# Splitting the last tile's down stage by tokens, with all weight blocks kept in SBUF

## Chip, cores, metric

The kernel runs on the 8 cores of one Trainium2 chip; each core computes one sequence of the batch. The metric is the device time of the slowest core, in microseconds (us). Executions come in a fast state and in a slow one, in which one die or both show a lower granted TensorE clock.

## The reference

Two layers of a decoder trunk, then one RMSNorm. What matters here is the very end of it:

```python
        y = modulate(rmsnorm(h, norm_g[l, 2]), sh3, sc3)
        h = h + 0.5 * g3[:, None, :] * swiglu(y, ffn2_wg[l], ffn2_wu[l], ffn2_wd[l])
    return rmsnorm(h, final_g)
```

`h` has 4096 positions of 1024 channels. The kernel holds it transposed, as 8 tiles of 512 tokens, each with 8 blocks (KC) of 128 channels. The hidden width 2816 is 22 blocks (FC).

## The kernel before

The program records tasks, a scheduler orders them per engine, and semaphores are emitted from the dependencies. The down stage of a tile is 8 groups of 22 matmuls; each group is followed by a residual add. `norm_out` is the final norm (cut to what matters):

```python
            def downs(self, tiles, dst={}, keep=True, lag=0):
                wd = {}
                for t in dst:
                    load_h(dst[t], t, self.src, self.bsrc, G.M)
                for m in range(KC + lag):
                    if m < KC:
                        wd[m] = load_wd(self.l, self.w, m, G.M)      # ring of 3 slots
                    for n, t in enumerate(tiles):                    # both tiles use the block in turn
                        k = m - lag * n
                        if 0 <= k < KC:
                            self.down(t, k, wd[k][0], wd[k][1], dst.get(t), keep)

        rsR = Ring([NM + 7168], [128, T], F32, "rstd")               # ONE buffer for the reciprocal norm
        # norm_sum: 8 squares (ACT), 7 sums (DVE or POOL), one mean matmul, logarithm, exp -> rs
        def norm_out(ht, t, pos, fine=False):
            rs, brs = norm_sum(ht, pos, 2 if fine else 0)
            for kc in range(KC):
                hk, bh = ht.ap[:, kc, :], ht.b[kc]
                fg = fg_sb[:, kc:kc + 1]
                G.op([dvex(lambda e, hk=hk, fg=fg: e.scalar_tensor_tensor(out=hk, in0=hk, scalar=fg, in1=rs, ...), 680)],
                     reads=[brs, bC["cst"]], writes=[bh], name="fin", pos=pos)
                ...                                                  # output DMA per block (fine) or per two

                # the end of the program
                hts = {6: HT(ACT[0]), 7: HT(ACT[1])}
                fc.downs((6, 7), hts, False, 1)
                norm_out(hts[6], 6, G.M, True)
                norm_out(hts[7], 7, G.M, True)
```

The softmax here doesn't subtract the row's maximum and nothing guards it: scores larger than these inputs give would overflow.

## Time and profile before

| | before |
|---|---|
| three timings | 5432.4, 5211.1, 4849.5 us (the first two slow) |
| profiled run, fast | 4873.3 us |
| from the last gate matmul to the end, die 0 | 169.9 to 170.4 us |
| of it after the last down matmul | 17.5 to 18.1 us |

The third row is read on each core from the end of the last gate matmul to the end of the execution. (A matmul ends its turn where the next one can start, 216 ns after its own start at 512 columns; its record ends some 0.17 us later.) On cores at full clock this stretch agrees to 0.1 us in the change and to 1.1 us in the kernel before, over two profiles of each, whereas the whole time moves by several us with the throttle. The view of spans and granted clocks of the kernel before shows that throttle even in a fast run; die 1, at a clock of 0.990, takes 40 us longer:

```profile
die 0 (median of its cores): 4824.8 us, clock 0.998
die 1 (median of its cores): 4864.5 us, clock 0.990
```

### The profile page before, as it was taken

What the parts mean: (1) busy time and instruction counts of PE and PEld (TensorE: products, weight loads), DVE (VectorE), ACT (ScalarE), POOL (GpSimd) and SP (SyncE); (2) the same over time, 40 slices, a digit from 0 to 9 for tenths busy, and PEclk for the clock granted to TensorE, in tenths of its full rate; (3) what the DMA queues carried; (4) which work ended last, traced back from release to release, by engine and by line L of the source; (5) the groups of instructions that cost most, each with busy time, mean ns of one, the idle gap of its engine ahead of it and who ended that gap; (6) DMA issues with size and microseconds to landing.
All of it is one profiled execution on the core that took longest, in us unless ns stands there. A gap on an engine that the chain in (4) does not pass through costs nothing.

```text
span 4871.8 us, 74168 instructions; the slowest of 8 cores (4820.7 to 4871.8 us)
## 1 busy us (share of the span) xinstructions
PE 4789.6 (98%) x25859; PEld 2257.4 (46%) x25859; DVE 2461.2 (51%) x4088; ACT 2035.0 (42%) x3024; POOL 973.5 (20%) x949
## 2 busy tenths in 40 slices
PE   6999999999999999999999999999999999999998
PEld 2444445444445554444444444444444455544443
DVE  6452566473655473655233326645537544525433
ACT  5112576452755352512211127645537444525311
POOL 0001551212531111300100026312235100122101
PEclk9999999999999999999999999999999999999999
DMA  8888676777575768755721466756665644473314
GB/s 240 169 191 230 166 204 159 191 206 218 172 209 150 200 192 240 218 147 165 249 66 39 120 200 163 208 155 184 149 190 164 185 148 140 123 248 124 136 42 157
DMA packets 370033, 834.80 MB, mean 171 GB/s; under 512 B 148961, under 2 KB 182113, under 8 KB 363234
## 3 DMA queue, kind: packets, MB, share of 16 engines
q1 hardware_dynamic: 352338, 741.56, 49.4%
q0 software_dynamic: 17328, 88.49, 12.1%
q8 instruction: 213, 3.49, 0.3%
q14 instruction: 154, 1.26, 0.1%
HBM read 741.20 MB, written 234.88 MB: 200 GB/s over the span
## 4 chain that ended last, share of the span: by engine, by line
PE 92%; ACT 2%; DMA 2%; DVE 2%; issue 1%; POOL 0%; SPq 0%; DVEq 0%; ACTq 0%; POOLq 0%
PE ps L1002 48%; PE ps L1030 25%; PE ps L1141 9%; PE ps L1467 5%; PE ps L1409 3%; PE ps L1375 2%; DMA arena<-xP 1%; DMA arena<-hS 0%; DVE arena L1206 0%; DVE arena L948 0%; POOL arena L1182 0%; DMA arena<-ada_w 0%; ACT arena L1184 0%; DMA arena<-wdS 0%; PE ps L1234 0%
## 5 line engine op out<-in xcount | busy, mean ns | idle before, releaser
L1002 PE MATMUL ps<-arena 128*128 128x512 bf16 x11264 | 2511.5, 381 | 32.6 <-DMA arena<-wgu 25.0
L1002 PEld LDWEIGHTS ps<-arena 128*128 128x128 bf16 x11264 | 1083.9, 98 | 1312.0 <-issue 86.4
L1030 PE MATMUL ps<-arena 128*128 128x512 bf16 x5632 | 1242.7, 382 | 1.1 <-DMA arena<-wdS 1.1
L1008 ACT ACTIVATE arena<-ps 128x512 f32<-128x512 f32 x704 | 419.7, 597 | 1283.7 <-PE ps L1002 1279.9
L1010 DVE SCALAR_TENSOR_TENSOR arena<-arena,ps 128x512 f32<-128x512 f32 x704 | 481.4, 685 | 771.9 <-ACT arena L1008 770.7
L1030 PEld LDWEIGHTS ps<-arena 128*128 128x128 bf16 x5632 | 550.7, 98 | 665.6 <-issue 47.9
L926 POOL TENSOR_TENSOR arena<-arena 128x512 f32<-128x512 f32 (+2 forms) x351 | 414.2, 1180 | 1218.4 <-ACT arena L919 1116.3
L1034 DVE SCALAR_TENSOR_TENSOR arena<-ps,arena 128x512 f32<-128x512 f32 x256 | 192.1, 751 | 908.3 <-PE ps L1030 899.9
L1015 DVE TENSOR_TENSOR arena<-ps,arena 128x512 bf16<-128x512 f32 x704 | 485.0, 690 | 216.6 <-PE ps L1002 193.3
L1141 PE MATMUL ps<-arena 128*128 128x512 bf16 x2560 | 577.1, 385 | 9.0 <-ACT arena L1225 5.8
L919 ACT ACTIVATE arena<-arena 128x512 bf16<-128x512 f32 x424 | 250.9, 625 | 709.1 <-DVE arena L1034 379.3
L1393 ACT ACTIVATE arena<-ps 128x1024 bf16<-128x1024 f32 (+1 forms) x384 | 344.9, 950 | 308.3 <-PE ps L1375 307.6
L1141 PEld LDWEIGHTS ps<-arena 128*128 128x128 bf16 x2560 | 251.0, 99 | 314.7 <-issue 52.0
L1396 DVE TENSOR_TENSOR arena<-arena 128x1024 bf16<-128x1024 bf16 (+1 forms) x384 | 256.1, 675 | 126.0 <-ACT arena L1393 124.6
L961 ACT ACTIVATE arena<-arena 128x512 bf16<-128x512 f32 x372 | 278.4, 806 | 45.2 <-DVE arena L948 45.1
L1445 POOL TENSOR_TENSOR arena<-arena 64x512 bf16<-64x512 f32 x128 | 163.8, 1280 | 623.1 <-ACT arena L1440 600.0
L948 DVE TENSOR_TENSOR arena<-arena 128x512 f32<-128x512 f32 x384 | 268.3, 747 | 35.0 <-ACT arena L934 32.0
L1467 PE MATMUL ps<-arena 128*128 128x512 bf16 x1024 | 230.1, 386 | 0.0
L1425 DVE TENSOR_TENSOR arena<-ps,arena 128x512 f32<-128x512 f32 x256 | 175.5, 685 | 65.2 <-PE ps L1409 57.5
L1409 PEld LDWEIGHTS ps<-arena 128*128 128x128 bf16 x2736 | 173.6, 98 | 63.4 <-issue 7.1
L1213 POOL TENSOR_TENSOR arena<-arena 128x512 bf16<-128x512 f32 x128 | 167.9, 1320 | 174.8 <-DVE arena L1204 120.2
L1409 PE MATMUL ps<-arena 128*128 128x128 bf16 x2736 | 194.4, 219 | 1.9 <-DVE arena L1010 0.9
(79 smaller groups left out, 2112.7 us busy)
## 6 DMA issues: line engine op xcount, KB each, us to landing
arena<-wguS SPq DMA_DIRECT2D x242, 512.0 KB, 5.7
arena<-hS SPq DMA_DIRECT2D x204, 512.0 KB, 6.8
arena<-wdS SPq DMA_DIRECT2D x128, 704.0 KB, 5.9
arena<-ada_w SPq DMA_DIRECT2D x144, 512.0 KB, 5.9
hS<-arena SPq DMA_DIRECT2D x224, 256.0 KB, 5.8
wguS<-wgu POOLq DMA_DIRECT2D x66, 512.0 KB, 7.8
hS<-arena SPq DMA_DIRECT2D x64, 512.0 KB, 4.3
arena<-xP SPq DMA_DIRECT2D x48, 512.0 KB, 9.0
```

The costliest lines, as they stand in the source:

```text
L926: f = lambda e, a=a, sq=sq, out=out: e.tensor_tensor(out=out, in0=a, in1=sq, op=ALU.add)
L948: f = lambda e, hk=hk, u=u: e.tensor_tensor(out=u, in0=hk, in1=rs, op=ALU.mult)
L961: ga = act(lambda e, hk=hk, A=A, sh=sh, o=o: e.activation(out=o, in_=hk, func=AF.Identity, scale=A, bias=sh), 725)
L1002: mate = main([(lambda e, kc=kc, half=half, bk=bk, y=y, gu=gu: e.matmul(bank(bk), lhsT=gu[:, half, kc, :], rhs=y[:, kc, :], start=(kc == 0 ...
L1008: G.op([act(lambda e, sg=sg, gb=gb: e.activation(out=smv[sg.i], in_=bank(gb), func=AF.Tanh, scale=0.5), 490, "tanh")], reads=[gb], writes= ...
L1010: G.op([dve(lambda e, sg=sg, gb=gb: e.scalar_tensor_tensor(out=smv[sg.i], in0=smv[sg.i], scalar=1.0, in1=bank(gb), op0=ALU.add, op1=ALU.mu ...
L1015: G.op([dve(lambda e, sg=sg, ub=ub, o=o: e.tensor_tensor(out=o, in0=bank(ub), in1=smv[sg.i], op=ALU.mult), 610)], reads=[ub, sg], writes=[ ...
L1030: main([(lambda e, j=j: e.matmul(bank(bk), lhsT=wd[:, j, :], rhs=a[:, j, :], start=(j == 0), stop=(j == FC - 1)), [bwd, ba[j]], MM) for j ...
L1141: ins.append((lambda e, lhs=lhs, rhs=rhs, kc=kc: e.matmul(bank(bk), lhsT=lhs, rhs=rhs, start=(kc == 0), stop=(kc == KC - 1)), rd + [by[kc] ...
L1393: return e.activation(out=cut(pT, 0), in_=cut(ps[:, :, :], sb.i * 512), func=AF.Exp, scale=0.125)
L1409: return e.matmul(o, lhsT=v[:, vi, h * 64:h * 64 + 128], rhs=pT[:, h, b, pc, :], start=(pc == 0 or not prev), stop=(pc == 1))
L1467: main([(lambda e, kc=kc, m=m, bk=bk: e.matmul(bank(bk), lhsT=w[:, m, kc, :], rhs=mx[:, kc, :], start=(kc == 0), stop=(kc == KC - 1)), [bw ...
```

## The change

The intent: tile 6 does its down stage first and alone, so that its norm and output lie beside tile 7's matmuls. Tile 7 then goes in parts of 256, 128 and 128 tokens, so that only the last part's norm and output remain when TensorE is done. For that all 8 weight blocks must stay in SBUF: five of them go into the space of the gate inputs (`Y0`), which is free by then.

```diff
-                hts = {6: HT(ACT[0]), 7: HT(ACT[1])}
-                fc.downs((6, 7), hts, False, 1)
-                norm_out(hts[6], 6, G.M, True)
-                norm_out(hts[7], 7, G.M, True)
+                h6, h7 = HT(ACT[0]), HP(ACT[1], ((0, 256), (256, 384), (384, 512)))
+                load_h(h6, 6, hS, bHS, G.M)
+                wd = [load_wd(l, 1, m, G.M + 4800.0 * m, None if m < 3 else Y0 + 5632 * (m - 3)) for m in range(KC)]
+                h7.load(7, hS, bHS, G.M + 30000.0)
+                for m in range(KC):
+                    fc.down(6, m, wd[m][0], wd[m][1], h6, False)
+                norm_out(h6, 6, G.M, 1)
+                for n in range(3):
+                    for m in range(KC):
+                        h7.down(fc, 7, n, m, wd[m][0], wd[m][1])
+                    h7.out(7, n, G.M)
```

Cut: the class `HP` (its `down` and `out` are `down` and `norm_out` on columns lo to hi, with an output DMA per two blocks), and limits in the scheduler that pace DMAs and reserve PSUM banks. With the values given these limits are never reached: the built programs hold the same order on every engine up to the last stage.

More of the change, by code (lines that the diff above doesn't have):

```diff
@@ L112, in _new @@
         t.mate = None
+        t.held = False
         t.banks, t.new = [], []
@@ L215 @@
     RESERVE = 2
+    PFAR, PLEN, PRATE = 1e9, 3000.0, 0.7
     def schedule(self, bw=270.0, dlat=2300.0, dmargin=3000.0, cmargin=250.0, backlog=9000.0):
@@ L227, in schedule @@
         pipe = [0.0]
+        pace = [0.0]
+        pes = []
         port = [0.0]
@@ L300, in pick @@
                         n = sum(b.n for b in t.new)
-                        if (t.pos > hp + 4000.0 or n > 1) and not (t.mate and t.mate.eng) and sum(x <= now for x in pfree["ps"]) < self.RESERVE + n:
-                            nxt = min(nxt, max(now + 50.0, sorted(pfree["ps"])[self.RESERVE + n - 1]))
+                        if (t.pos > hp + 4000.0 or n > 1) and not (t.mate and t.mate.eng) and sum(x <= now for x in pfree["ps"]) < (7 if n == 6 else self.RESERVE + n):
+                            nxt = min(nxt, max(now + 50.0, sorted(pfree["ps"])[(7 if n == 6 else self.RESERVE + n) - 1]))
                             continue
@@ L331, in pick @@
                         nxt = min(nxt, max(pipe[0] - bl, now + 50.0) if bl == backlog else now + 200.0)
+                        continue
+                    if far > self.PFAR and now > 100000.0 and pace[0] - now > self.PLEN:
+                        t.held = True
+                        nxt = min(nxt, max(pace[0] - self.PLEN, now + 100.0))
                         continue
@@ L396, in schedule @@
             t.start, t.dur = st, dur
+            if e == "pe":
+                pes.append(t)
+            if t.dma and t.held:
+                x = next((x for x in reversed(pes) if x.end + 100.0 <= now), None)
+                if x is not None:
+                    t.deps = t.deps | {x}
             if t.dma:
+                pace[0] = min(max(pace[0], now) + t.nbytes / (bw * self.PRATE), max(now + 8000.0, pipe[0] + t.nbytes / bw))
                 pipe[0] = max(pipe[0], st + dur) + t.nbytes / bw
@@ L846, in load_gu, with load_wd @@
             return ap, b
-        def load_wd(l, w, m, pos):
-            o = WD0 + 5632 * (wdn[0] % 3)
-            wdn[0] += 1
+        def load_wd(l, w, m, pos, o=None):
+            if o is None:
+                o = WD0 + 5632 * (wdn[0] % 3)
+                wdn[0] += 1
             ap, b = tile(o, [128, FC, 128], BF16, 1, "wd")
@@ L977, in norm_out, with __init__, load, down @@
                                         262144 * (kc - k0 + 1), reads=ht.b[k0:kc + 1], name="out", pos=pos))
+        class HP:
+            def __init__(self, off, parts):
+                self.ap = view(off, [128, KC, T], F32)
+                self.parts = parts
+                self.b = [[reg(off + 2048 * kc + 4 * a, off + 2048 * kc + 4 * b, "h") for kc in range(KC)] for a, b in parts]
+            def load(self, t, src, bsrc, pos):
+                for q in range(4):
+                    G.dma("sp", lambda e, q=q: e.dma_start(out=self.ap[:, 2 * q:2 * q + 2], in_=src[t, :, 2 * q:2 * q + 2]), 524288,
+                          reads=bsrc[t][2 * q:2 * q + 2], writes=[x for b in self.b for x in b[2 * q:2 * q + 2]], name="hld", pos=pos)
+            def down(self, ffn, t, n, m, wd, bwd):
+                a, ba = ffn.act[t]
+                lo, hi = self.parts[n]
+                bk = Bank()
+                o, b = self.ap[:, m, lo:hi], self.b[n][m]
+                main([(lambda e, j=j: e.matmul(bank(bk)[:, 0:hi - lo], lhsT=wd[:, j, :], rhs=a[:, j, lo:hi], start=(j == 0),
+                                               stop=(j == FC - 1)), [bwd, ba[j]], (hi - lo) / 2.4 + 2.7) for j in range(FC)],
+                     [bk], "down", [])
+                g = (ffn.l * 3 + ffn.i) * KC + m
+                G.op([dve(lambda e: e.scalar_tensor_tensor(out=o, in0=bank(bk)[:, 0:hi - lo], scalar=Gv[:, g:g + 1], in1=o,
+                                                           op0=ALU.mult, op1=ALU.add), 120 + 1.07 * (hi - lo))],
+                     reads=[bk, bMod[ffn.l][ffn.i][1]], writes=[b], name="resid", pos=G.M)
+            def out(self, t, n, pos):
+                lo, hi = self.parts[n]
+                w = hi - lo
+                (s, bs), (sb, bsb), (rs, brs) = smR.take(), sbR.take(), rsR.take()
+                s, sb, rs = s[:, 0:w], sb[:, 0:w], rs[:, 0:w]
+                prev = None
+                for kc in range(KC):
+                    sq, bq = sqR.take()
+                    sq = sq[:, 0:w]
+                    hk = self.ap[:, kc, lo:hi]
+                    G.op([act(lambda e, sq=sq, hk=hk: e.activation(out=sq, in_=hk, func=AF.Square), 200 + 0.63 * w)],
+                         reads=[self.b[n][kc]], writes=[bq], name="sq", pos=pos)
+                    if kc == 0:
+                        prev = (sq, bq)
+                        continue
+                    a, ba = prev if kc == 1 else (s, bs)
+                    o, bo = (sb, bsb) if kc == KC - 1 else (s, bs)
+                    f = lambda e, a=a, sq=sq, o=o: e.tensor_tensor(out=o, in0=a, in1=sq, op=ALU.add)
+                    G.op([dvex(f, 90 + 1.03 * w)], reads=[ba, bq], writes=[bo], name="sqsum", pos=pos)
+                bk = Bank()
+                G.chain([(lambda e: e.matmul(bank(bk)[:, 0:w], lhsT=mean_bf, rhs=sb, start=True, stop=True), [bsb, bC["mean"]],
+                          w / 2.4 + 2.7)], [bk], "nsum", pos=pos)
+                G.op([act(lambda e: e.activation(out=rs, in_=bank(bk)[:, 0:w], func=AF.Ln, bias=eps_sb), 250 + 0.66 * w, "ln")],
+                     reads=[bk, bC["eps"]], writes=[brs], name="ln", pos=pos)
+                G.op([act(lambda e: e.activation(out=rs, in_=rs, func=AF.Exp, scale=-0.5), 200 + 0.64 * w, "exp")], reads=[brs],
+                     writes=[brs], name="rexp", pos=pos)
+                for kc in range(KC):
+                    hk, fg = self.ap[:, kc, lo:hi], fg_sb[:, kc:kc + 1]
+                    G.op([dvex(lambda e, hk=hk, fg=fg: e.scalar_tensor_tensor(out=hk, in0=hk, scalar=fg, in1=rs, op0=ALU.mult,
+                                                                             op1=ALU.mult), 110 + 1.11 * w)],
+                         reads=[brs, bC["cst"]], writes=[self.b[n][kc]], name="fin", pos=pos)
+                    if kc % 2:
+                        G.outs.append(G.dma("sp", lambda e, kc=kc: e.dma_start(out=outP[t, :, kc - 1:kc + 1, lo:hi],
+                                                                              in_=self.ap[:, kc - 1:kc + 1, lo:hi]),
+                                            1024 * w, reads=self.b[n][kc - 1:kc + 1], name="out", pos=pos))
```

## The prediction

> **What bounds the kernel now.** The page comes first: it says which engine sets the span.
>
> ```profile
> PE 4789.6 (98%) x25859; PEld 2257.4 (46%) x25859; DVE 2461.2 (51%) x4088; ACT 2035.0 (42%) x3024; POOL 973.5 (20%) x949
> ...
> PE 92%; ACT 2%; DMA 2%; DVE 2%; issue 1%; POOL 0%; SPq 0%; DVEq 0%; ACTq 0%; POOLq 0%
> ```
>
> TensorE is busy 98% of the span and carries 92% of the chain of waits. A change can only pay where it lets TensorE finish earlier or shortens what follows its last matmul. The change touches the last stage alone, so next I read the busy time by stretch there: tiles 4 and 5 (4701 to 4777 us), tiles 6 and 7 (to 4854.25), and what is left (columns: PE, its weight loads PEld, DVE, ACT, POOL, granted clock, DMA share, GB/s).
>
> ```profile
> 4701.00:4777.00 76.00, 76.00 (x354) 34.47 (x353) 12.15 (x17) 7.96 (x13) 9.59 (x9) 1.00 0.28 84
> 4777.00:4854.25 77.25, 77.25 (x356) 34.75 (x354) 30.90 (x44) 15.03 (x24) 7.72 (x7) 0.99 0.44 155
> 4854.25:4862.20 7.95, 0.76 (x3) 0.10 (x1) 6.74 (x10) 1.79 (x3) 0.00 (x0) 0.83 0.50 173
> 4862.20:4871.80 9.60, 0.00 (x0) 0.00 (x0) 5.39 (x8) 1.32 (x2) 0.00 (x0) 0.50 0.84 295
> ```
>
> Through both down stages TensorE never idles. From 4854.25 to 4871.8 it does almost nothing: 17.55 us in which the final norm and output of tiles 6 and 7 run one after the other. The timeline of that stretch, in order (start, length, engine, line):
>
> ```profile
> 4802.02 52.40 PE L1030 MATMUL ps<-arena 128*128 128x512 bf16 x242
> ...
> 4854.52 0.75 DVE L1034 SCALAR_TENSOR_TENSOR arena<-ps,arena 128x512 f32<-128x512 f32 x1 [1.68 <-PE ps L1030]
> 4854.73 0.69 ACT L932 ACTIVATE arena<-ps,arena 128x512 f32<-128x512 f32 x1 [3.41 <-PE ps L930]
> 4855.36 0.63 ACT L919 ACTIVATE arena<-arena 128x512 bf16<-128x512 f32 x1
> 4855.90 0.61 ACT L934 ACTIVATE arena<-arena 128x512 f32<-128x512 f32 x1
> 4856.10 0.69 DVE L926 TENSOR_TENSOR arena<-arena 128x512 bf16<-128x512 f32 x1 [0.82 <-ACT arena L919]
> 4856.70 5.38 DVE L970 SCALAR_TENSOR_TENSOR arena<-arena 128x512 f32<-128x512 f32 x8
> ...
> 4856.94 0.38 PE L930 MATMUL ps<-arena 128*128 128x512 bf16 x1 [2.31 <-DVE arena L926]
> 4857.52 12.02 SPq L975 DMA_DIRECT2D outP<-arena  x16
> 4862.24 0.69 ACT L932 ACTIVATE arena<-ps,arena 128x512 f32<-128x512 f32 x1 [5.73 <-DVE arena L970]
> 4863.02 0.63 ACT L934 ACTIVATE arena<-arena 128x512 f32<-128x512 f32 x1
> 4863.75 5.39 DVE L970 SCALAR_TENSOR_TENSOR arena<-arena 128x512 f32<-128x512 f32 x8 [1.66 <-ACT arena L934]
> ```
>
> The last residual add (L1034), square (L919), sum (L926) and mean matmul (L930) of tile 7 are over by 4857.3. Its logarithm (L932) then waits 5.73 us for DVE: there is one buffer for the reciprocal norm, and tile 6 uses it until its eight scalings (L970) end. Then come exp, tile 7's own eight scalings (5.39 us), and 2.66 us until the last output has landed.
>
> **What the Trainium skill says.** "TensorE: Matmul & The Clock Gate", section "Back-to-back issue gap", gives N/2.4 + 2.5 ns for one matmul, but for a stream of weight load and matmul pairs says 81 ns at N=128 and 131 ns at N=512. The trace disagrees with the second pair: 242 matmuls in 52.4 us are 216 ns each at 512 columns, every one with its own weight load. At 128 columns there are bursts in attention:
>
> ```profile
> 714.52 1.06 PE L1409 MATMUL ps<-arena 128*128 128x128 bf16 x16
> 715.42 1.89 PE L1002 MATMUL ps<-arena 128*128 128x512 bf16 x8
> ```
>
> Sixteen are issued in 0.90 us, 56 ns each, although each has its own weight load. "VectorE: DVE Perf Modes", section "The TRN2 errata", says that an instruction pays a fixed latency and gives (N+151)/0.96 ns for an fp32 add; at 512 that is 691, and L926 measures 692 on DVE. So I scale VectorE by 1.04 ns per column. "DMA: Bandwidth & Descriptors", section "Anatomy of one DMA", puts about 2.0 us fixed on a transfer, mostly the receipt of the write; the 2.66 us from the last scaling to the end agree, so smaller outputs will not remove it.
>
> **The change part by part.** The built programs of before and after hold the same order on every engine until the last stage; the new pacing limits in the scheduler are never reached. So nothing before about 4701 us moves.
>
> (1) Tile 6 does its whole down stage first, then tile 7 in parts of 256, 128, 128 tokens. Tile 6's norm and outputs, whose eight scalings now hold up tile 7's logarithm for 5.73 us, then lie beside tile 7's 38 us of matmuls: hidden. So do the norms of tile 7's first two parts.
>
> (2) Tile 7's 176 matmuls of 512 columns (176 x 0.216 = 38.02 us) become 176 of 256 and 352 of 128. The line through 216 at 512 and 56 at 128 gives 109.3 ns at 256: 19.24 + 352 x 0.056 = 19.71, together 38.95 us, so +0.93 on the path. Three mean matmuls now stand in front of the last main matmul (0.216 + 0.109 + 0.056): +0.38. Sum +1.31.
>
> (3) The tail after the last main matmul, at 128 columns. Residual add: starts 0.27 later as now; 0.34 (the list of groups by shape has a 128x128 one from PSUM, L1122, at 336 ns). Square: ACT loses about 0.85 ns per column (L783 1060 ns at 1024, L919 625 at 512), so 0.30; sum 0.29; mean matmul 0.22; logarithm 0.36; exp 0.30. The six gaps from one instruction's end to the next one's start, read off the lines above, are 0.10, 0.10, 0.15, 0.10, 0.09 and 0.10, together 0.64. That is 0.27 + 0.34 + 0.30 + 0.29 + 0.22 + 0.36 + 0.30 + 0.64 = 2.72 us. Eight scalings: now one every 0.673 us (5.39/8), less 384 columns x 1.04 ns gives 0.27; eight make 2.26 with the longer last one. Landing: 2.6, barely less than the 2.66. Tail 7.58 us.
>
> (4) Saving: 17.55 - 7.58 - 1.31 = 8.66 us, 0.18% of the span. I take off 0.5 for small waits: 8.2.
>
> (5) Eight weight blocks in SBUF: five go into the space of the gate inputs, free from 4701 on, so they load while DMA is 28% busy. No time, unless late (rival B).
>
> **Rivals.** A: weight loads bound the narrow matmuls. With the skill's 81 ns, 352 x 25 ns = 8.8 us come back and the saving is nil. For it: the page and PEld's 98 ns records; bursts of 352 are longer than any of 16 here. Against: at 56 ns those 98 ns records already overlap. I give it one in eight.
>
> B: a weight block comes late. Tile 6 alone uses 704 KB every 4.75 us instead of every 9.5. The third block reuses the slot that tile 5's last group frees at 4777 and is needed 9.5 us later; tile 6's 2 MB of residual are issued just before it, tile 7's 2 MB just after. Alone it takes some 5.9 us from issue (the page's figure for these blocks); if it shares the some 380 GB/s, which the transfer view shows in its busy slices around 4780, with all of that, about 9 us. TensorE could wait 0 to 2 us: saving 6 to 8.
>
> C: VectorE falls behind. A 128-token group gives a bank every 22 x 56 ns = 1.23 us; VectorE owes it one add (0.34), one sum (0.29) and, in four of eight groups of the second part, two 256-wide scalings (0.81): 1.44 us. It lags for four groups, then catches up, and the spare banks cover it. The mean matmul of each part stands two groups behind it (2.46 us), and its inputs need about 1.6. A stall here costs under 1 us.
>
> D: the machine's state hides it. The three timings are 4849.5, 5211.1 and 5432.4 us; the profiled run, fast, took 4873.3. The slow state is worth 40 times the change.
>
> **Range and chances.** Against the fast runs (4849.5 timed, 4873.3 profiled with one die at clock 0.99), 8.2 us less is 4841 to 4865; I put 4846, nearer the timed one. Fast runs alone should lie within 4825 and 4875. Two of three timings before were slow, though, so a median of a few runs may be a slow one; the range to hold in 8 of 10 cases reaches to 5250 for that reason only. In equal state nothing here is worth 2% (97 us): faster by over 2% 0.01, within 2% 0.97, slower by over 2% 0.02.
>
> **What would show it.** Right: the order before 4701 unchanged; the 128-wide down matmuls 56 ns apart; no idle of TensorE over 0.5 us in tile 7; the logarithm of the last part waiting for its matmul, not for VectorE's scalings; eight scalings in about 2.3 us; 7 to 8.5 us from the last main matmul to the end, against 17.55. Wrong: down groups of 128 taking over 1.5 us each (A), TensorE waiting on the third block's transfer (B), or mean matmuls waiting over 1 us for VectorE (C); a saving under 4 us or over 11 in equal state would mean that my sum has a wrong term.

## The result, and the profile after

The ratio is the mean time of one kernel's fast runs over that of the other's of the same rounds, so it is not quite the ratio of the medians.

| | before | change |
|---|---|---|
| median of 6 runs, states mixed | 4915.7 us | 4840.2 us |
| fast runs | 4849.5, 4852.9, 4846.8 | 4838.6, 4840.4, 4836.8, 4840.1 |
| ratio of fast runs | | 0.9978, 95% interval 0.9958 to 0.9997 |
| last gate matmul to end, die 0 | 169.9 to 170.4 | 160.8 |
| matmuls of tiles 6 and 7 (full clock) | 76.41 | 77.67 |
| tail after the last down matmul | 17.5 to 18.8 | 7.16 to 7.19 |

In equal state it is 0.2% faster, within 2%. The spans and clocks of the change: die 1 was throttled less than in the profile before, so the two pages' spans (4871.8 and 4837.0) must not be subtracted from each other.

```profile
die 0 (median of its cores): 4818.2 us, clock 0.999
die 1 (median of its cores): 4828.7 us, clock 0.996
```

TensorE's own timeline of the last stage, on the slowest core: L1108 is tile 6 (after tiles 4 and 5), L1013 is tile 7 in parts, L946 and L1041 are the mean matmuls of the norms.

```profile
4776.36 14.41 PE L1108 MATMUL ps<-arena 128*128 128x512 bf16 x66
4790.60 4.97 PE L1013 MATMUL ps<-arena 128*128 128x256 bf16 x44
4795.40 0.38 PE L946 MATMUL ps<-arena 128*128 128x512 bf16 x1
4795.62 17.03 PE L1013 MATMUL ps<-arena 128*128 128x256 bf16 x176
4812.49 0.27 PE L1041 MATMUL ps<-arena 128*128 128x256 bf16 x1
4812.60 9.99 PE L1013 MATMUL ps<-arena 128*128 128x128 bf16 x176
4822.42 0.22 PE L1041 MATMUL ps<-arena 128*128 128x128 bf16 x1
4822.48 7.53 PE L1013 MATMUL ps<-arena 128*128 128x128 bf16 x132
4831.41 0.22 PE L1041 MATMUL ps<-arena 128*128 128x128 bf16 x1 [1.40 <-DVE arena L1038]
```

Two things are to be seen. No line but the last has a bracket (the view prints one for an idle time above 0.15 us), so TensorE never idles for longer than that: no late weight block, no mean matmul that waits for its sum. And 176 matmuls of 128 columns take 9.82 us (4812.60 to 4822.42), 56 ns each, in a run of matmuls eleven times longer than the bursts I had. (The view names a merged line by its first form: the `x176` before it are 132 matmuls of 256 and the next part's first 44 of 128, as the mean matmul stands two groups behind its part.)

The timeline of all engines after the last down matmul, which ends its turn at 4829.8:

```profile
4830.12 0.35 DVE L1017 SCALAR_TENSOR_TENSOR arena<-ps,arena 128x128 f32<-128x128 f32 x1
4830.56 0.31 ACT L1031 ACTIVATE arena<-arena 128x128 bf16<-128x128 f32 x1 [0.92 <-DVE arena L1017]
4830.98 0.29 DVE L1038 TENSOR_TENSOR arena<-arena 128x128 bf16<-128x128 f32 x1 [0.51 <-ACT arena L1031]
...
4831.73 0.37 ACT L1043 ACTIVATE arena<-ps,arena 128x128 f32<-128x128 f32 x1 [0.85 <-PE ps L1041]
4832.19 0.31 ACT L1045 ACTIVATE arena<-arena 128x128 f32<-128x128 f32 x1
4832.60 2.19 DVE L1049 SCALAR_TENSOR_TENSOR arena<-arena 128x128 f32<-128x128 f32 x8 [1.33 <-ACT arena L1045]
```

It is the chain of before at a quarter of the width: add, square, sum, mean matmul, logarithm, exp, eight scalings. The logarithm (L1043) now waits for its mean matmul and not for VectorE's scalings. The end comes at 4837.0, 2.2 us after the last scaling; this last stretch, in which the output is issued, written and checked, is called the landing.

### The profile page after: what moved, and what is told of

It is laid out like the page before. It is cut to its first block, busy times and chain, and to the rows that moved or that the text cites. A ratio compares the mean times of both kernels' runs of the same rounds, so it can differ in the third digit from the quotient of the medians.

```text
span 4837.0 us, 75013 instructions; the slowest of 8 cores (4814.6 to 4837.0 us)
## 1 busy us (share of the span) xinstructions
PE 4763.3 (98%) x26213; PEld 2270.6 (47%) x26213; DVE 2470.8 (51%) x4134; ACT 2040.0 (42%) x3044; POOL 974.8 (20%) x949
## 3 DMA queue, kind: packets, MB, share of 16 engines
q14 instruction: 154, 1.26, 0.1%
## 4 chain that ended last, share of the span: by engine, by line
PE 92%; ACT 3%; DMA 2%; DVE 2%; issue 1%; POOL 0%; SPq 0%; DVEq 0%; ACTq 0%; POOLq 0%
PE ps L1080 49%; PE ps L1108 24%; PE ps L1219 8%; PE ps L1545 5%; PE ps L1487 3%; PE ps L1453 2%; DMA arena<-xP 1%; PE ps L1013 1%; DMA arena<-hS 1%; DVE arena L964 0%; ACT arena L1262 0%; DVE arena L1284 0%; POOL arena L1260 0%; DMA arena<-wdS 0%; PE ps L1312 0%
## 5 line engine op out<-in xcount | busy, mean ns | idle before, releaser
L1080 PE MATMUL ps<-arena 128*128 128x512 bf16 x11264 | 2503.0, 380 | 33.1 <-DVE arena L970 26.0
L1080 PEld LDWEIGHTS ps<-arena 128*128 128x128 bf16 x11264 | 1082.2, 98 | 1305.9 <-issue 58.8
L1108 PE MATMUL ps<-arena 128*128 128x512 bf16 x5456 | 1198.1, 381 | 0.9 <-DMA arena<-wdS 0.9
L1108 PEld LDWEIGHTS ps<-arena 128*128 128x128 bf16 x5456 | 531.9, 98 | 639.6 <-issue 26.5
L1219 PE MATMUL ps<-arena 128*128 128x512 bf16 x2560 | 570.6, 381 | 8.8 <-ACT arena L1303 6.1
L1219 PEld LDWEIGHTS ps<-arena 128*128 128x128 bf16 x2560 | 249.3, 98 | 309.9 <-issue 31.5
L1545 PE MATMUL ps<-arena 128*128 128x512 bf16 x1024 | 224.6, 379 | 0.0
L1487 PEld LDWEIGHTS ps<-arena 128*128 128x128 bf16 x2736 | 173.5, 98 | 63.3 <-issue 6.8
```

Source lines behind the costliest of these rows:

```text
L1080: mate = main([(lambda e, kc=kc, half=half, bk=bk, y=y, gu=gu: e.matmul(bank(bk), lhsT=gu[:, half, kc, :], rhs=y[:, kc, :], start=(kc == 0 ...
L1108: main([(lambda e, j=j: e.matmul(bank(bk), lhsT=wd[:, j, :], rhs=a[:, j, :], start=(j == 0), stop=(j == FC - 1)), [bwd, ba[j]], MM) for j ...
L1219: ins.append((lambda e, lhs=lhs, rhs=rhs, kc=kc: e.matmul(bank(bk), lhsT=lhs, rhs=rhs, start=(kc == 0), stop=(kc == KC - 1)), rd + [by[kc] ...
L1487: return e.matmul(o, lhsT=v[:, vi, h * 64:h * 64 + 128], rhs=pT[:, h, b, pc, :], start=(pc == 0 or not prev), stop=(pc == 1))
L1545: main([(lambda e, kc=kc, m=m, bk=bk: e.matmul(bank(bk), lhsT=w[:, m, kc, :], rhs=mx[:, kc, :], start=(kc == 0), stop=(kc == KC - 1)), [bw ...
```

## The experiments

Which half of the gain comes from where, and which cost sets the widths? My theory is the sum of the prediction: the order (tile 6 first) and the split each remove about half of the tail, and narrow matmuls of n columns cost only n/2.4 + 2.7 ns, the line through the 216 ns at 512 columns and the 56 ns at 128 that the traces show. The rivals are named in each expectation. All outputs were correct. (In the expectations "from tile 5's last group" is the sum of the matmuls of tiles 6 and 7 and the tail; the 76.0 us of tiles 4 and 5 come on top for "from the last gate matmul". The runs with a chip on record were made on five chips; the stage may be compared across them, as far as the two profiles of the change tell, which agree in it to 0.1 us.)

| kernel | matmuls 6 and 7 | tail | last gate matmul to end |
|---|---|---|---|
| before | 76.41 | 17.5 to 18.1 | 169.9 to 170.4 |
| before again | 76.41 | 17.5 to 18.6 | 169.9 to 171.0 |
| change | 77.67 | 7.17 | 160.8 |
| change again | 77.67 | 7.15 to 7.29 | 160.8 to 160.9 |
| one part of 512 | 76.62 | 13.6 | 166.2 |
| 256, 256 | 77.17 | 9.17 | 162.3 |
| 384, 128 | 77.22 | 7.7 to 7.9 | 160.9 to 161.1 |
| 256, 192, 64 | 77.69 | 7.56 | 161.2 |
| blocks loaded again | 109.0 to 111.2 | 7.2 | 192.1 to 195.1 |
| before, second norm buffer | 76.41 | 16.4 to 17.4 | 168.8 to 169.7 |
| change, batched scalings | 77.67 | 7.05 | 160.7 |
| 384, 128, batched, two buffers | 77.22 | 7.3 to 7.5 | 160.5 to 160.7 |
| 256, 192, 64, two buffers | 77.69 | 6.88 | 160.5 |
| 256, 192, 64, batched, two buffers | 77.69 | 7.0 to 7.1 | 160.6 to 160.7 |
| change, early checks | 77.67 | 7.16 to 7.23 | 160.8 to 160.9 |
| 256, 192, 64, two buffers, early checks | 77.69 | 8.1 to 8.2 | 161.8 to 161.9 |

(The matmul column is from cores on which no record of the last down stages is missing. The row of the blocks loaded again is die 0, where the clock fell below 0.97 in this stage.)

### The order alone

```diff
-HP(ACT[1], ((0, 256), (256, 384), (384, 512)))
+HP(ACT[1], ((0, 512),))
```

> The changed kernel with tile 7 in one part of 512: tile 6 still goes first, nothing is split. I count from the end of tile 5's last down group. Sum theory (both halves of the change pay): the tail after the last main matmul falls from about 17.6 us to about 13.0 (add 0.75, square 0.63, sum 0.69, mean matmul 0.38, logarithm 0.69, exp 0.63, gaps 0.91, scalings 5.4, landing 2.9), the matmuls before it take 76.6 us on an unthrottled die, so about 89.6 us in all, halfway between before (94.2) and the change (84.9). Rival (order alone: the gain is only that tile 6's scalings no longer stand in front of tile 7's logarithm, and the split is given back by narrow matmuls): as fast as the change, about 85 us.

The end of it, in the timeline of a core at full clock:

```profile
4813.54 0.69 ACT L1043 ACTIVATE arena<-ps,arena 128x512 f32<-128x512 f32 x1 [1.42 <-PE ps L1041]
4814.32 0.63 ACT L1045 ACTIVATE arena<-arena 128x512 f32<-128x512 f32 x1
4815.05 5.39 DVE L1049 SCALAR_TENSOR_TENSOR arena<-arena 128x512 f32<-128x512 f32 x8 [2.13 <-ACT arena L1045]
```

The logarithm's wait of 5.7 us is gone, but one tile's eight scalings of 5.39 us remain. Measured 76.62 + 13.6 = 90.2 us from tile 5's last group, against 89.6 (sum theory) and 85 (order alone). So the order is worth some 4 us and the split 5.4 more (166.2 to 160.8). The 0.6 us by which I missed are the landing: the last output, 512 KB here, is over 3.5 us after the last scaling, where I had put 2.9. The timings of the whole kernel (1.0019, interval 0.9886 to 1.0153, one fast run with a die at clock 0.99) are too wide to say anything.

### Two equal parts

```diff
-((0, 256), (256, 384), (384, 512))
+((0, 256), (256, 512))
```

> The changed kernel with tile 7 in two parts of 256. Sum theory: the tail scales with the width of the last part, about 9.1 us (2.6 with the first wait up to the mean matmul's end, 1.5 to the first scaling, eight scalings 3.3, landing 2.4), the matmuls 77.2 us, 86.3 in all, 1.4 us slower than the change. Rival (the narrow matmuls cost as much as the split gives): equal to the change or faster.

77.17 + 9.17 = 86.3 us, the sum to the tenth: the tail shrinks with the width of the last part (13.6 us at 512, 9.17 at 256, 7.17 at 128), and two matmul sets of 128 columns cost 0.5 us more than one of 256. The whole kernel's ratio to before was 0.9975, interval 0.9932 to 1.0018.

### 384 and 128

```diff
-((0, 256), (256, 384), (384, 512))
+((0, 384), (384, 512))
```

> The changed kernel with tile 7 in parts of 384 and 128: the same width at the end, but one set of 128-wide matmuls fewer. Sum theory: matmuls 77.3 us instead of 77.7, tail 7.2, 84.4 in all, 0.4 us faster than the change. Rival (VectorE falls behind: in the last 9.9 us it has to do eight scalings of 384 columns, 4.3 us, beside 4.8 us of the last part's own work): the scalings of the first part are not over when the last part's add is due, the tail grows to 8 to 9 us and it is 0.5 to 1.5 us slower than the change.

Neither quite: the matmuls are 0.45 us shorter as the sum says, the tail is 0.55 us longer as the rival says, and the total is the same as the change within 0.1 to 0.3 us. Last lines of its timeline:

```profile
4812.09 0.35 DVE L1017 SCALAR_TENSOR_TENSOR arena<-ps,arena 128x128 f32<-128x128 f32 x1
4812.35 1.14 DVE L1049 SCALAR_TENSOR_TENSOR arena<-arena 128x384 f32<-128x384 f32 x2
...
4813.41 0.29 DVE L1038 TENSOR_TENSOR arena<-arena 128x128 bf16<-128x128 f32 x1
4813.84 0.22 PE L1041 MATMUL ps<-arena 128*128 128x128 bf16 x1 [1.97 <-DVE arena L1038]
```

The last sum (L1038) stands behind two scalings of the 384 part, which VectorE has not finished yet; TensorE's last mean matmul waits 1.97 us for it, against 1.40 in the change. So the width of the part before the last is limited by what VectorE can scale beside the last part's own adds and sums.

### 256, 192 and 64

```diff
-((0, 256), (256, 384), (384, 512))
+((0, 256), (256, 448), (448, 512))
```

> The changed kernel with tile 7 in parts of 256, 192 and 64. Sum theory with the line n/2.4 + 2.7 ns for every width: the matmuls of 64 columns are 29 ns apart, the matmul stage takes 77.8 us, the tail about 6.3 us, 84.1 in all, 0.8 us faster than the change. Rival (weight loads set a floor that 128 columns just meet): they are 53 to 56 ns apart, the stage takes 4.4 us more, about 88.5 in all, slower than the change by 3.6 us.

The matmul term holds: 88 matmuls of 64 columns in a row were 29 ns apart, each with its own weight load of 128 columns, and the stage took 77.69 us (expected 77.8, floor theory 82.2). No floor by weight loads down to 64 columns. But the tail did not shrink to 6.3; it grew to 7.56:

```profile
4806.43 1.07 DVE L1049 SCALAR_TENSOR_TENSOR arena<-arena 128x192 f32<-128x192 f32 x3
4806.65 0.19 PE L1041 MATMUL ps<-arena 128*128 128x64 bf16 x1 [1.51 <-DVE arena L1038]
4807.65 0.31 ACT L1043 ACTIVATE arena<-ps,arena 128x64 f32<-128x64 f32 x1 [1.71 <-DVE arena L1049]
```

A group of 64 columns lasts 22 x 29 = 0.64 us. For each, VectorE has an add (0.28), a sum (0.21) and a scaling of the part before (0.41) to do. Their records overlap, and it starts such a trio every 0.66 us: it just keeps pace and has no time to catch up. The scalings of the part before can start only after its exp, well inside the last part, so three of them are left at the end, and the logarithm waits for them through the single norm buffer: the wait of the kernel before, back again in small.

### Are the kept weight blocks needed?

```diff
-                for m in range(KC):
-                    fc.down(6, m, wd[m][0], wd[m][1], h6, False)
+                for m in range(KC):
+                    wd, bwd = load_wd(l, 1, m, G.M)          # ring of 3, for tile 6; tile 7's residual is loaded at m == 5
+                    fc.down(6, m, wd, bwd, h6, False)
...
                     for m in range(KC):
-                        h7.down(fc, 7, n, m, wd[m][0], wd[m][1])
+                        wd, bwd = load_wd(l, 1, m, G.M)      # and again for each part of tile 7
+                        h7.down(fc, 7, n, m, wd, bwd)
```

> The changed kernel with the weight blocks not kept: three slots as before, and every part of tile 7 loads all eight blocks again. If keeping them matters (5.77 MB per part, at some 380 GB/s 15 us against 9.9 us of matmuls in a part of 128): TensorE waits on transfers of the blocks in tile 7 for 8 to 15 us, and the total from tile 5's last group is 93 to 100 us, so the gain of the split is gone. If the DMA has room for it: TensorE does not wait and it takes 85 us, as the change.

This profile was slow; I read die 0, whose clock was 0.997. The waits of TensorE in the last stage on its core 0:

```profile
PE ps L1013 <- DMA arena<-wdS: 22.4, 15, 4.1
PE ps L1108 <- DMA arena<-wdS: 0.2, 1, 0.2
```

22.4 us of waiting for blocks, all but 0.2 in tile 7, in 15 waits. From tile 5's last group it took 116 us, more than before. So the direction is as expected and the size is larger. I had not counted the outputs of tiles 4 to 6, which share the DMA (the windows view has it 77 to 100% busy from tile 6 on), nor that a ring of three runs no further ahead than three blocks; what each of them costs was not tested. Some 6 us more, by my estimate from the bursts in TensorE's timeline, are longer matmuls: the windows view shows a granted clock of 0.93, 0.93 and 0.85 in tile 7, and single groups of 128 columns took 1.99 and 2.08 us there instead of 1.39. That the idle time between them lowered the clock is not shown. With a ring of three the split loses more than it gains; a deeper ring was not tried.

### The kernel before with a second norm buffer

```diff
                 norm_out(hts[6], 6, G.M, True)
+                rsR.offs[:] = [ACT[0] + 16384]
                 norm_out(hts[7], 7, G.M, True)
```

> The kernel before, with a second buffer for the reciprocal norm, used by tile 7 alone: the 5.73 us wait of its logarithm for tile 6's scalings is gone, nothing else is changed. If that wait is worth its length: the tail falls by 5 to 6 us, from 17.6 to about 12. If VectorE's queue is the real bound (tile 6's eight scalings stand in front of tile 7's anyway): only the logarithm, exp and two gaps, 1.5 to 1.7 us, leave the path, tail about 16.

```profile
4815.25 10.68 DVE L970 SCALAR_TENSOR_TENSOR arena<-arena 128x512 f32<-128x512 f32 x16
...
4816.07 10.27 SPq L975 DMA_DIRECT2D outP<-arena  x16
4816.17 0.69 ACT L932 ACTIVATE arena<-ps,arena 128x512 f32<-128x512 f32 x1 [1.11 <-PE ps L930]
```

The 5.7 us wait is gone and the logarithm runs early, yet the tail falls only from 17.5 to 18.1 down to 16.4 to 17.3 (die 0). VectorE does sixteen scalings without a gap; they were the bound, not the wait that the profile names. Tile 7's scalings no longer wait 1.66 us for the logarithm and exp, but the outputs take half of that back (mean tail on die 0 from 17.7 to 16.9): the last lands 3.3 to 4.2 us after the last scaling, as sixteen of them now follow each other without a pause.

### Fewer scaling instructions, and the norm buffer

ScalarE applies the gain in advance; VectorE then multiplies four, two and two blocks by the reciprocal norm, broadcast. The outputs are regrouped with it, four, two and two blocks instead of four times two:

```diff
-                for kc in range(KC):                          # 8 x scalar_tensor_tensor(h * fg * rs)
+                for kc in range(KC):                          # on ScalarE, ahead of time: h = h * fg
+                    G.op([act(lambda e, hk=hk, fg=fg: e.activation(out=hk, in_=hk, func=AF.Identity, scale=fg), ...)], ...)
+                for a, b in ((0, 4), (4, 6), (6, 8)):         # on VectorE: h = h * rs, rs broadcast over blocks
+                    f = lambda e, a=a, b=b: e.tensor_tensor(out=self.ap[:, a:b, lo:hi], in0=self.ap[:, a:b, lo:hi],
+                                                            in1=cust(rs, 0, [[0, b - a], [1, w]]), op=ALU.mult)
```

> The changed kernel, but ScalarE multiplies each block by the final gain ahead of time, so that VectorE's scaling needs the reciprocal norm alone and does four, two and two blocks in one instruction each, instead of eight. Theory (each VectorE instruction costs some 0.13 us over its columns): the last scalings take 1.55 us instead of 2.19, the tail 6.5 us instead of 7.17; 160.2 us from the last gate matmul to the end instead of 160.8. Rival (a broadcast operand or the extra ScalarE work costs as much): tail 7.2 or more.

```profile
4810.68 0.31 ACT L1045 ACTIVATE arena<-arena 128x128 f32<-128x128 f32 x1
4811.09 1.36 DVE L1052 TENSOR_TENSOR arena<-arena 128x512 f32<-128x512 f32 x3 [1.33 <-ACT arena L1045]
```

The scalings took 1.36 us instead of 2.19, even less than expected, but the tail fell by 0.12 us only. From the last scaling to the end it is now 2.93 us instead of 2.23: in the trace the last output is issued 0.41 us after its scaling (0.07 in the change), as the queue is still issuing the one before, and it lands 2.23 us after that instead of 1.87. (The end comes 0.29 us after that in both.) A gain on VectorE that the outputs gave back.

The same with parts of 384 and 128, and two norm buffers in turn (`rsR.offs[:] = [ACT[0] + 16384, ACT[1] + 16384]`):

> Parts of 384 and 128, batched scalings, two buffers for the reciprocal norm used in turn. Theory (the tail of 7.7 us with parts of 384 and 128 was VectorE's lag behind the scalings of 384 columns): with 3.3 us instead of 4.3 of them the lag goes, tail 6.5 us, matmuls 77.2, from the last gate matmul 159.7 us. Rival (VectorE's order is the matter, not its amount): tail stays at 7 or above, 160.2 us or more.

Tail 7.3 to 7.5, total 160.5 to 160.7, as the rival says: the last mean matmul still waits 1.73 us for its sum, against 1.97 without batching, and the landing again took most of what the shorter scalings gave (2.9 us instead of 2.2).

Parts of 256, 192 and 64 with two norm buffers and nothing batched:

> Parts of 256, 192 and 64 with two buffers for the reciprocal norm, nothing batched. There the last logarithm waited 1.71 us for VectorE's scalings, as in the kernel before. If that wait is what lengthened the tail to 7.56 us: it falls to 6.3. If the scalings that stand in front in VectorE's queue do (as with the second buffer in the kernel before): by 0.7 us only, to about 6.9, 160.5 us from the last gate matmul.

6.88 us, the number of the second theory, but not for its reason. The logarithm no longer waits (it starts 0.1 us after its mean matmul), and the last scalings wait for the exp, not for the three late ones, which end 0.21 us before:

```profile
4814.95 1.66 DVE L1049 SCALAR_TENSOR_TENSOR arena<-arena 128x64 f32<-128x64 f32 x8 [0.21 <-ACT arena L1045]
```

What is left of the lag lies earlier: the last sum stands behind two late scalings, and the last mean matmul waits 1.50 us for it. The landing, 2.50 us, is longer than in the change too.

Both together:

> Parts of 256, 192 and 64, batched and with two buffers. If fewer instructions relieve VectorE: tail 6.2 us or less, 159.8 us from the last gate matmul. If a block of 64 columns (0.65 us of matmuls) is below what VectorE and ScalarE need for one block in any case: the tail stays near 6.9 and it is no better than parts of 384 and 128.

Tail 7.0 to 7.1: batching does not help on top. The last scalings take 0.83 us instead of 1.66, but the sums of the last part now stand behind larger scalings (the last mean matmul waits 2.24 us instead of 1.50) and the end comes 2.7 us after the last scaling. Whether another order on VectorE would help at 64 columns was not tried.

### What sets the last 2.2 us?

At the very end the queue checks the semaphores of all outputs one after another, 0.05 us each. The edit checks all but the last four before the last part's first output is issued:

```diff
             if t.dma:
+                if t is self.outs[-4]:
+                    for x in self.outs[:-4]:
+                        wait(e, x)
                 waits(e, t.deps)
```

> The changed kernel, but the queue checks the earlier outputs (24 semaphores) before it issues the last part's first output instead of at the very end, where they take 0.05 us each, 1.3 us in a row, before the last one is waited for. If the landing of the last output is what the end waits for (in the profile of the change the checks end 0.1 us ahead of it): the end comes 0 to 0.1 us earlier, last scaling to end 2.15 to 2.25 us. If the row of checks is the floor: 0.4 us or more earlier, 1.8 us or less.

Unchanged, 2.23 us: the landing of the last output is the floor, not the checks.

> Parts of 256, 192 and 64 with two norm buffers and the same early checks. There the row of checks ran back to back up to the end, so the landing of the last output was not seen. If the checks were the floor: from the last scaling to the end falls from 2.50 us to 2.2 or less, tail 6.5, 160.2 us from the last gate matmul, the best of all. If outputs of 64 columns (rows of 256 bytes) land no earlier: it stays at 2.4 to 2.5.

The edit spoiled its own test: the stretch went from 2.5 to 3.8 us. With a last part as short as this the outputs of the 192 part are still in flight when the checks are made, so the queue waits for them before it issues anything. (This profile was slow too; the cores of its undisturbed die agree within 0.1 us.) Whether outputs of 64 columns land earlier can be read all the same. The DMA views of the change and of the parts of 256, 192 and 64 with two norm buffers (core 0) give the median from issue to landing in the last column:

```profile
outP<-arena SPq DMA_DIRECT2D x8, 128.0 KB, 1.9
outP<-arena SPq DMA_DIRECT2D x4, 64.0 KB, 1.7
```

They do, by 0.2 us, but that did not reach the end: the last one is issued 0.41 us after its scaling instead of 0.07, and the row of checks ends after it has landed.

### The two kernels again

> The changed kernel again, unedited, in five rounds against the kernel before. My text said 8.2 us less in equal state (ratio 0.9983); the stage read from the two profiles says about 9.5 us (ratio 0.9980). If the first rounds' ratio of 0.9978 is right, it comes out between 0.997 and 0.999. If the difference between the medians (4915.72 and 4840.24 us) were the change's doing and not the state's, it would come out near 0.985.

Of the six runs of the change one was fast, 4824.1 us, against five fast runs of before from 4833.0 to 4836.7 (mean 4835.3); a ratio with an interval was not to be had. That single pair is 0.9977, inside what I expected, far from the 0.985 of the medians. The stage of the change came out at 160.8 us again.

> The kernel before once more, for a second profile of it, since one die of its first profile ran at clock 0.99. If the first profile stands for the kernel, the cores take 169.9 to 170.4 us from the last gate matmul to the end at full clock, 9.1 to 9.6 us more than the 160.8 us of the change, and the last output lands 2.6 to 4.0 us after the last scaling, at random, where the change has 2.23 on nearly every core. If the throttled die was not typical and the change saves 11 us at full clock, as the fast timings of the whole kernel say, it is 171.8 us.

On its unthrottled cores 169.9 to 171.0 us, with the last landing 2.6 to 3.7 us after the last scaling. So the first profile stands, and the change saves 9.1 to 10.2 us, depending on that landing.

## Why the prediction was right or wrong

**The single number was wrong as a forecast, by the step "Range and chances".** I took 4846 us from the fast runs, while the time that it stands beside, 5211.1 us, was a slow run's, the median of three of which two were slow. Read against that median, 4846 says 7% faster, which no step of the sum says. What the runs showed in its place is 0.2%: 10.8 us between the means of the fast runs, 9.1 to 10.2 us in the stage. The text itself named 8.2 us in equal state, put fast runs between 4825 and 4875 (measured 4836.8 to 4840.4) and gave 0.97 to "within 2%", and that came true. But a number of one state set against a median of another is a forecast of the state. The six-run medians repeat the error with measured numbers: 4915.7 and 4840.2 differ by 1.5%, of which fast runs show 0.2%.

**The mechanism held, term by term:**

| step | predicted | measured |
|---|---|---|
| order unchanged before the last stage | yes | yes |
| longer matmul stage | +1.31 us | +1.26 (77.67 less 76.41) |
| 128-column matmuls | 56 ns | 56 ns |
| last matmul to first scaling | 2.72 | 2.75 |
| eight scalings | 2.26 | 2.19 |
| last scaling to end | 2.6 | 2.23 |
| tail | 7.58 | 7.17 |
| saving in equal state | 8.66, less 0.5 | 9.1 to 10.2 by the stage; 10.8 by the means of the fast runs, interval 1.5 to 20 |

Two terms were mis-sized. The 0.5 us for small waits did not exist: no wait of TensorE in tile 7 stands in its timeline. And I took the landing over from before almost unchanged, and from core 5, which had one of the shortest: 2.65 us, where the cores of the two profiles of before had 2.6 to 4.0 (eight outputs of 256 KB, one every 0.66 us). The change has 2.2 on nearly every core, with four of 128 KB. The prediction's "smaller outputs will not remove it" rests on the fixed 2.0 us alone. The cited section of the Trainium skill ("DMA: Bandwidth & Descriptors", "Anatomy of one DMA") adds the bytes at 436 GB/s to it, an estimate of 0.3 us less for half of 256 KB; and its fit is made for the gpsimd path, while these outputs are issued by SyncE. The runs agree with the second part, at 0.29 us. From issue to landing the last output took 3.2 us with 512 KB (one part of 512), 2.16 with 256 KB (two of 256), 1.87 with 128 KB and 1.69 with 64 KB.

One reading of the profile was incomplete, without harm to the sum: the prediction puts the tail before down to the wait for the norm buffer, 5.73 us. The second norm buffer shows that VectorE's queue of sixteen scalings was the bound. The change takes tile 6's scalings out of the tail, so both go at once.

**Rival A** (weight loads bound narrow matmuls) is refuted at 128 columns by the change and at 64 by the run with a last part of 64. **Rival B** (a late weight block) did not show: no wait. Without kept blocks it is the bound, 22.4 us. **Rival C** (VectorE behind) did not hurt at 256, 128, 128, where the mean matmuls two groups later found their sums ready; it is what the next narrower choices run into. **Rival D** (the state hides it) is what the timings of a whole kernel show: most timed executions were slow, by 100 to 980 us.

The 0.6 to 1.7 us between the stage's saving and that of the fast timings are not explained; they are well inside the interval.

**A better version?** The best stage time of all, 160.5 us (256, 192, 64 with two norm buffers), is 0.3 us below the change, less than 0.01% of the time. No timing here could show it, so I do not claim it. Among the widths tried, the split by 256, 128, 128 sits on a flat optimum: a narrower last part moves the limit to VectorE, a faster VectorE moves it to the landing of the output.

## What to carry to other kernels

What follows the last matmul is paid in full, and here it shrank with the width of the last piece: split the last piece by its independent axis, keep its weights resident, and stop where the engine behind TensorE needs longer for a piece than TensorE does. A wait that the profile names can stand in front of another on the same engine: the 5.7 us wait for the norm buffer was worth about 1 us, because VectorE's queue was full either way. And when executions have two states, forecast and compare in one of them, or on the part of the program that the change touches.

## What the Trainium skill lacked or had wrong

- "TensorE: Matmul & The Clock Gate", section "Back-to-back issue gap": it gives a sustained 81 ns at N=128 and 131 ns at N=512 for weight load and matmul pairs. Here pairs sustain 56 ns at 128 columns over 352 matmuls and 216 ns at 512; 64 columns, also with a weight load each, 29 ns. Its formula N/2.4 + 2.5, called the isolated gap there, is what the stream shows. (The page's section "Wait — 56ns, not 53.3ns?" does give 55.6 and 215.7 ns for matmuls back to back.)
- "DMA: Bandwidth & Descriptors", section "Anatomy of one DMA", written for the gpsimd path: its fit of 2.0 us plus the bytes at 436 GB/s gives estimates of 2.2, 2.3, 2.6 and 3.2 us for 64, 128, 256 and 512 KB; the outputs here, issued by SyncE, took 1.69, 1.87, 2.16 and 3.2 us from issue to landing. The page has no figure for how this landing grows when the outputs before it follow closely: 2.23 us in the batched kernel, whose last three outputs (512 KB in all) were issued within 1.0 us, against 1.6 us for the last four in the change. Its section "Latency and other measured facts" says in general that a lighter HBM load makes the fixed cost smaller.
- "VectorE: DVE Perf Modes", section "The TRN2 errata": (N+151)/0.96 ns for an fp32 add holds at widths that the page does not list: 0.29 us at 128 columns (291 by the formula), 0.42 at 256 (424).
